# A mixer layer with three attention branches: the 630 DMAs that are not transposes are issued from GpSimd's queue instead of SyncE's

## The chip, the core and the metric

The kernel runs on one core of one Trainium2 chip. The metric is the device time of one execution in microseconds (us). TensorE (PE in the rows) multiplies; its weight loads have rows of their own (PEld). VectorE is DVE, ScalarE is ACT, GpSimd is POOL. SyncE (SP) computes nothing: it issues DMAs, one after the other, and a DMA that waits for something holds up those behind it in the same queue. GpSimd's queue works the same way, but has arithmetic in it as well.

## The reference

One layer of width 1024 over 2048 tokens. The normalised input goes through one wide projection; its columns feed three causal attention branches, a SiLU path for each, and 3072 sigmoid gates:

```python
h = rmsnorm(x, norm_g[l])
proj = h @ w_in[l]
...
pd = p[:, :, 0] - lam * p[:, :, 1]            # differential attention, 4 heads of two maps
s = s + c[:, :, start:end, None] - c[:, :, None, :end]   # forgetting attention, 8 heads
DIL_PATTERNS = ((128, 1), (512, 4), (2048, 16))          # dilated windows, 8 heads
...
y = jnp.stack([ya, yb, yc], axis=2)           # each times silu(its z columns)
branch = jnp.einsum('bsne,nef->bsnf', y, w_branch[l])
merged = jnp.sum(gates * branch, axis=2)
x = x + merged @ w_out[l]
return rmsnorm(x, final_g)
```

## The kernel before

Every product is made in f16 from a high and a low half, so a projection of 128 columns by 512 tokens is 24 matmuls. The work goes through twelve groups of 128 columns of attention output: groups 0 to 3 are differential, 4 to 7 forgetting, 8 to 11 dilated. A tail follows (branch projections, gates, output projection, final norm). In the profile the start and groups 0 and 1 take up to some 280 us, the other differential groups run to about 900 us, the forgetting ones to 1680, the dilated ones to 2380, and the tail to the end.

Inside a group, score jobs are interleaved with projection work for this group and the next (value, SiLU path, gates, query and key). The order of each engine's instructions is set by a scheduler from the program and its own estimates of durations. Tiles come from pools with few slots, and an instruction that writes into a used slot waits for the slot's last reader.

A score job: TensorE makes the scores (L661, L662; L1095, L1098 in dilated groups), VectorE adds the bias and takes the maximum into a tile `e` (L696, L1109), ScalarE takes the exponential (L710, L1118), both split it into halves (L727, L728), a DMA transpose brings it into `eT` (L736), and TensorE multiplies it by the values (L718, L721). There are 5 slots for `e` and 6 for `eT`.

All DMAs are issued from SyncE's queue, `Q`. The transposes are those of `eT`, of the values `v` (L546), of the SiLU path `zt` (L574) and, in the tail, of `u` (L1321). The other DMAs are weight loads `w` (L324, 3 slots; VectorE takes their maximum next, L304), gate stores `gd` (L594, from 3 slots `gs` that the `v` and `z` evictions use too), copies `q2` of query halves (L668, L669, L1004, L1005), the row of decays `R` (L942), outputs `ud` (L1231), loads `gt`, `w_b`, `wo` of the tail, and four kinds of the dilated groups: values to DRAM and back in strided order (`vd` L549, then `v1` L1038 and `v2` L1040), results of the strided patterns to DRAM (`od` L1155, from 3 slots that hold `ro` and `o`), their statistics (`sp` L1170) and their loads back (`o1`, `o2`, L1195). Loads of x, stores of the result and a few small ones have a place of their own in the program and are not touched.

GpSimd's arithmetic: it adds the halves of `zt` into `z` (L575), masks a bias tile `bl` for each forgetting job (L964), copies statistics into `ro` (L1146), and after each group multiplies and adds what finishes it. After a dilated group g that is `post_dil`, which runs beside the jobs of group g+1: eight rounds of multiplying `y` (L1192) and the loaded `o1` and `o2` (L1197), adding them (L1198), and a product with `z` every second round (L1213). Only when it is over can the next group's `z` be written, since `y` and `z` share 3 slots.

Of the kernel before, what the change touches and what calls it, by code (L numbers as in the profile page):

```python
# [19 lines left out]
P = 128  # L20
# [136 lines left out]
def tile_hybrid_trunk(  # L157
# [14 lines left out]
    V, A, G, T, Q = nc.vector, nc.scalar, nc.gpsimd, nc.tensor, nc.sync  # L172

# [145 lines left out]
    def w_load(pieces, name):  # L319
        wt = w_tile(f"w_{name}")  # L320
        stg = wt[:, 256:].rearrange("p (k c) -> p k c", k=KC)
        o = 0
        for c, w in pieces:
            Q.dma_start(stg[:, :, o:o + w], w2[:, c:c + w].rearrange("(k p) c -> p k c", p=P))  # L324
            o += w
        return wt
# [202 lines left out]
    def fill_v(gr):  # L529
# [3 lines left out]
        for t4 in range(4):  # L533
# [13 lines left out]
            if gr["br"] == 2:  # L547
                for a in range(2):
                    Q.dma_start(gr["vd"][512 * t4:512 * t4 + 512, a].rearrange("(b p) c -> p b c", p=P), vt[:, 4 * a:4 * a + 4])  # L549
# [33 lines left out]
    def gate_unit(i, tg):  # L583
# [10 lines left out]
        Q.dma_start(gd[i // 4][i % 4][:, 512 * tg:512 * tg + 512], t)  # L594
# [69 lines left out]
    def make_q2(gr, u, i):  # L664
# [3 lines left out]
        Q.dma_start(t[0:64], stk[64:128, 0, ts])  # L668
        Q.dma_start(t[64:128], stk[0:64, 0, ts])  # L669
# [265 lines left out]
    def prologue_fox(gr):  # L935
        gr["R"] = []
        for u in range(2):
# [4 lines left out]
            Q.dma_start(R, csd[NB * h:NB * h + NB].rearrange("b t -> (b t)").unsqueeze(0).to_broadcast([P, S]))  # L942
# [56 lines left out]
    def prologue_dil(gr):  # L999
        i = gr["i"]  # L1000
        q2 = []
        for u in range(2):
            t = e_tile(f"q2_{gr['n']}_{u}", (P, S), F16)
            Q.dma_start(t[0:64], gr["stk"][u][64:128, 0])  # L1004
            Q.dma_start(t[64:128], gr["stk"][u][0:64, 0])  # L1005
# [23 lines left out]
    def load_v_dil(gr):  # L1029
        gr["vp"] = [None, None, None]  # L1030
        for p in (1, 2):
# [3 lines left out]
            if p == 1:  # L1035
                vs = gr["vd"].rearrange("(j x c r) a e -> j c x (r a e)", j=4, c=4, r=d)
                for j in range(4):
                    Q.dma_start(vv[:, j], vs[j])  # L1038
            else:
                Q.dma_start(vv[:, 0], gr["vd"].rearrange("(i r) a c -> i (r a c)", r=d))  # L1040
            gr["vp"][p] = vt

    def jobs_dil(gr):
# [17 lines left out]
        def job(p, bs):  # L1061
# [59 lines left out]
            def T_():  # L1121
                eh = transpose_tile(hold["e"], widths, 2.0 ** 14, name)

                def pv():
                    seen = set()
                    for h in range(0, len(bs), 2):
# [24 lines left out]
                        if p > 0:  # L1151
# [3 lines left out]
                            Q.dma_start(v, ro)  # L1155
# [10 lines left out]
    def post_dil(gr):  # L1166
        y, s1, n = gr["y"], gr["s1"], gr["n"]
        sp = bl_tile(f"sp_{n}").rearrange("p (a b c) -> p a b c", a=2, c=4)
        for p in (1, 2):
            Q.dma_start(sp[:, p - 1], gr["od"][p].rearrange("(b p) c -> p b c", p=P)[:, :, P:P + 4])  # L1170
# [17 lines left out]
        for i in range(8):  # L1188
# [4 lines left out]
            for p in (1, 2):  # L1193
                o = ro_tile(f"o{p}_{n}_{i}")[:, :256].rearrange("p (b c) -> p b c", b=2)
                Q.dma_start(o, gr["od"][p].rearrange("(b p) c -> p b c", p=P)[:, sl, :P])  # L1195
# [5 lines left out]
    def post(gr):  # L1201
# [25 lines left out]
        for t4 in range(4):  # L1227
# [3 lines left out]
            Q.dma_start(ud[gr["br"]][:, t4, gr["i"]], yh[:, ts])  # L1231
# [93 lines left out]
    def load_gate(n):  # L1325
        if n < 24:
            j, tg = divmod(n, 4)
            gts[n] = xpool.tile([P, 4, 512], F32, tag=f"xT1_{tg}", name=f"gt_{n}")
            Q.dma_start(gts[n], gd[j][:, :, 512 * tg:512 * tg + 512].rearrange("f p t -> p f t"))
# [9 lines left out]
    def prep_b(br, j):  # L1339
# [3 lines left out]
        Q.dma_start(sf.rearrange("p (k c) -> p k c", k=4), w_branch[0, br, :, 256 * j:256 * j + 256].rearrange("(k p) c -> p k c", p=P))  # L1343
# [93 lines left out]
    def load_out(c):  # L1437
        t = w_tile(f"wo_{c}") if c < W_SLOTS else e_tile(f"wo_{c}", (P, 1280))
        j, a = divmod(c, 2)
        Q.dma_start(t[:, 256:].rearrange("p (k c) -> p k c", k=4), w_out[0, 512 * a:512 * a + 512, 256 * j:256 * j + 256].rearrange("(k p) c -> p k c", p=P))  # L1440
# [237 lines left out]
```

## Time and profile before

| what | us |
|---|---|
| median of 3 runs | 2783.12 (2778.27 to 2783.22) |
| the profiled execution | 2802.34 |
| its span, first to last instruction | 2800.6 |

The profiled execution lies 19 us above the median of the runs; every duration below is from it. A busy share is an average over stages with different limits, so stages are read apart. A wait is booked to what ended last before it.

### The profile page before, as it was taken

How to read it: one execution, taken by the hardware profiler on the slowest of the kernel's cores; microseconds unless marked ns; L12 is line 12 of the kernel's file. 1: busy time of each engine (PE TensorE's matmuls, PEld its weight loads, DVE VectorE, ACT ScalarE, POOL GpSimd, SP SyncE). 2: the span in 40 equal slices, each digit the busy share in tenths (PEclk: the TensorE clock that was granted, in tenths of full speed). 3: DMA queues.
4: the chain of work that ended last, by engine and by line, in shares of the span. 5: the costliest groups of instructions: out<-in, count | busy, mean ns of one | idle time of the engine just before them, and what ended most of it. 6: DMA issues, size and time to landing. Idle time of an engine off the chain costs nothing.

```text
span 2800.6 us, 48432 instructions
## 1 busy us (share of the span) xinstructions
PE 2634.3 (94%) x16264; PEld 1378.4 (49%) x16264; DVE 2088.7 (75%) x7120; ACT 1669.5 (60%) x3642; POOL 383.4 (14%) x565
## 2 busy tenths in 40 slices
PE   7999999999999999999999998998979887999998
PEld 4455445455455444454455444544545444444555
DVE  8687978977977868778778776667667665678855
ACT  6466666656566666666676656756758577435311
POOL 0000200200102102102111120132041310400000
PEclk9899999989999999999999999998989998999999
DMA  4345445444455787887886878679687799764222
GB/s 159 74 88 111 89 92 108 99 83 110 90 105 112 140 162 143 159 156 148 150 167 131 153 137 145 133 149 162 138 158 156 139 204 230 212 187 137 95 100 76
DMA packets 981834, 377.02 MB, mean 135 GB/s; under 512 B 842824, under 2 KB 939856, under 8 KB 980048
## 3 DMA queue, kind: packets, MB, share of 16 engines
q1 hardware_dynamic: 981584, 373.93, 63.3%
q8 instruction: 127, 2.08, 0.3%
q14 instruction: 123, 1.01, 0.1%
HBM read 118.14 MB, written 59.05 MB: 63 GB/s over the span
## 4 chain that ended last, share of the span: by engine, by line
PE 58%; DVE 13%; DMA 12%; ACT 8%; issue 5%; SPq 2%; POOL 1%; DVEq 0%; ACTq 0%; POOLq 0%
PE pq_g L385 12%; PE pg L385 11%; PE pbr L385 9%; DMA eT_g<-e_g 6%; PE pz_g L385 5%; PE pout L1485 4%; PE po_g L718 3%; PE pv_g L385 3%; PE s_g L661 3%; PE s_g L662 3%; ACT e_g L1118 2%; DVE e_g L728 2%; PE pout L1486 2%; DVE e_g L696 2%; PE po_g L721 2%
## 5 line engine op out<-in xcount | busy, mean ns | idle before, releaser
L385 PE MATMUL pg<-xT,w_g 128*128 128x512 f16 x2304 | 582.9, 394 | 4.4 <-ACT gs L593 2.8
L710 ACT ACTIVATE e_g<-e_g,nm_g,c_g 128x1024 f32<-128x1024 f32 (+7 forms) x384 | 377.6, 984 | 251.4 <-DVE nm_g L704 218.4
L385 PE MATMUL pq_g<-xT,w_q 128*128 128x512 f16 x1536 | 388.4, 399 | 15.5 <-DVE stk_g L416 14.8
L728 DVE SCALAR_TENSOR_TENSOR e_g<-e_g 128x512 f16<-128x512 f32 (+2 forms) x480 | 316.4, 669 | 89.0 <-ACT e_g L727 86.4
L718 PE MATMUL po_g<-v_g,eT_g 128*128 128x128 f16 (+1 forms) x2232 | 315.4, 236 | 34.6 <-DMA eT_g<-e_g 16.8
L385 PEld LDWEIGHTS <-w_g 128*128 128x128 f16 x2304 | 223.6, 101 | 244.3 <-issue 13.9
L727 ACT ACTIVATE e_g<-e_g 128x512 f16<-128x512 f32 (+2 forms) x480 | 265.9, 569 | 91.3 <-DVE e_g L728 86.7
L385 PE MATMUL pz_g<-xT,w_z 128*128 128x512 f16 x1152 | 288.4, 390 | 6.5 <-DVE stk_g L416 5.3
L721 PE MATMUL po_g<-v_g,eT_g 128*128 128x64 f16 (+1 forms) x2232 | 293.6, 201 | 0.0
L385 PE MATMUL pv_g<-xT,w_v 128*128 128x512 f16 x1152 | 283.2, 395 | 2.8 <-DVE vs_g L545 1.4
L1118 ACT ACTIVATE e_g<-e_g,nm_g,c_g 128x256 f32<-128x256 f32 (+1 forms) x384 | 207.8, 543 | 111.0 <-DVE nm_g L1114 109.0
L385 PE MATMUL pbr<-u,w_b 128*128 128x512 f16 x1152 | 264.9, 393 | 4.1 <-ACT gs L593 1.9
L718 PEld LDWEIGHTS <-eT_g 128*128 128x128 f16 x2232 | 211.2, 100 | 87.0 <-DMA eT_g<-e_g 25.2
L661 PE MATMUL s_g<-stk_g 128*128 128x512 f16 (+3 forms) x640 | 228.1, 358 | 25.1 <-DVE pm_g L696 24.7
L721 PEld LDWEIGHTS <-eT_g 128*128 128x128 f16 x2232 | 206.5, 99 | 78.7 <-issue 21.7
L385 PEld LDWEIGHTS <-w_q 128*128 128x128 f16 x1536 | 148.7, 102 | 178.1 <-DVE stk_g L416 16.7
L696 DVE CUSTOM_DVE_ANT_0 e_g<-s_g,bias_g 128x512 f32<-128x512 f32 (+3 forms) x320 | 190.3, 605 | 60.8 <-DMA eT_g<-e_g 39.1
L662 PE MATMUL s_g<-stk_g,q_g 128*128 128x512 f16 (+3 forms) x640 | 229.0, 360 | 0.2 <-issue 0.2
L696 DVE CUSTOM_DVE_ANT_0 e_g<-s_g,R_g 128x512 f32<-128x512 f32 (+3 forms) x288 | 171.5, 597 | 43.9 <-DMA eT_g<-e_g 29.7
L385 PEld LDWEIGHTS <-w_b 128*128 128x128 f16 x1152 | 115.3, 100 | 146.6 <-issue 8.1
L385 PEld LDWEIGHTS <-w_v 128*128 128x128 f16 x1152 | 114.8, 101 | 134.9 <-issue 7.9
L1485 PE MATMUL pout<-wo,acc 128*128 128x512 f16 x512 | 172.7, 389 | 0.0
(476 smaller groups left out, 4331.7 us busy)
## 6 DMA issues: line engine op xcount, KB each, us to landing
gd<-gs SPq DMA_DIRECT2D x96, 256.0 KB, 2.7
gt<-gd SPq DMA_DIRECT2D x24, 1024.0 KB, 5.2
w_g<-in_w_in_dram SPq DMA_DIRECT2D x24, 512.0 KB, 4.1
ud<-y_g SPq DMA_DIRECT2D x48, 256.0 KB, 3.1
eT_g<-e_g SPq DMA_TRANSPOSE x640, 3.2
od_g<-ro_g SPq DMA_DIRECT2D x64, 132.0 KB, 2.3
xb<-in_x_dram SPq DMA_DIRECT2D x16, 512.0 KB, 6.5
q_g<-stk_g SPq DMA_DIRECT2D x128, 64.0 KB, 2.3
```

What stands on the lines that cost most here:

```text
L385: T.matmul(dst, l, r, start=(i == 0), stop=(i == n - 1))
L661: behind_read(T.matmul(ps, stk[:, 0, qsl], stk[:, 1, ksl], start=True, stop=False))
L662: T.matmul(ps, q2s, stk[:, 1, ksl], start=False, stop=True)
L696: rd = V.tensor_tensor_reduce(out=et[ch // 2][:, o + a:o + a + sw], in0=ps[:, a:a + sw], in1=b, scale=1.0, scalar=-3e38, op0=ALU.add, op1= ...
L710: A.activation(e[:, 256:256 + w], e[:, 256:256 + w], AF.Exp, bias=nm, scale=gr["c"][u], accum_out=den_of(i))
L718: ins = T.matmul(po, eh, vv, start=first, stop=False)
L721: T.matmul(po[:, 0], el, vv[:, 0], start=False, stop=last)
L727: A.activation(h[:, :w], f, AF.Copy, scale=scale)
L728: V.scalar_tensor_tensor(h[:, w:], f, scale, h[:, :w], op0=ALU.mult, op1=ALU.subtract)
L1118: A.activation(eu, eu, AF.Exp, bias=nm[:, 2 * a + u:2 * a + u + 1], scale=gr["c"][u], accum_out=sm[:, a, 2 + u:3 + u])
L1485: T.matmul(po, ah, wo[un][k], start=k == 0, stop=False)
L1486: T.matmul(po[:, 0], al, wo[un][k][:, 0], start=False, stop=k == KC - 1)
```

## The change

A name `RQ` for GpSimd's DMA queue is added, and the DMAs named above that are not transposes are issued through it: 630 of the 1437. What they move, and what waits for them, stays the same. The loads of x, `dl`, `g8`, `fw`, `fb`, `gb`, `fg`, the store `csd`, the stores of the result and all transposes stay with SyncE.

```diff
--- before.py
+++ after.py
@@ -170,6 +170,7 @@
     V, A, G, T, Q = nc.vector, nc.scalar, nc.gpsimd, nc.tensor, nc.sync
+    RQ = nc.gpsimd
 
@@ -321,7 +322,7 @@
         for c, w in pieces:
-            Q.dma_start(stg[:, :, o:o + w], w2[:, c:c + w].rearrange("(k p) c -> p k c", p=P))
+            RQ.dma_start(stg[:, :, o:o + w], w2[:, c:c + w].rearrange("(k p) c -> p k c", p=P))
             o += w
@@ -546,7 +547,7 @@
                 for a in range(2):
-                    Q.dma_start(gr["vd"][512 * t4:512 * t4 + 512, a].rearrange("(b p) c -> p b c", p=P), vt[:, 4 * a:4 * a + 4])
+                    RQ.dma_start(gr["vd"][512 * t4:512 * t4 + 512, a].rearrange("(b p) c -> p b c", p=P), vt[:, 4 * a:4 * a + 4])
                 if t4 == 3:
@@ -591,7 +592,7 @@
             A.activation(t, pd, AF.Copy)
-        Q.dma_start(gd[i // 4][i % 4][:, 512 * tg:512 * tg + 512], t)
+        RQ.dma_start(gd[i // 4][i % 4][:, 512 * tg:512 * tg + 512], t)
 
@@ -665,8 +666,8 @@
         ts = slice(512 * i, 512 * i + 512)
-        Q.dma_start(t[0:64], stk[64:128, 0, ts])
-        Q.dma_start(t[64:128], stk[0:64, 0, ts])
+        RQ.dma_start(t[0:64], stk[64:128, 0, ts])
+        RQ.dma_start(t[64:128], stk[0:64, 0, ts])
         return t
@@ -939,7 +940,7 @@
             R = bias_tile(f"R_{gr['n']}_{u}")
-            Q.dma_start(R, csd[NB * h:NB * h + NB].rearrange("b t -> (b t)").unsqueeze(0).to_broadcast([P, S]))
+            RQ.dma_start(R, csd[NB * h:NB * h + NB].rearrange("b t -> (b t)").unsqueeze(0).to_broadcast([P, S]))
             A.activation(R, R, AF.Copy, scale=nic)
@@ -1001,8 +1002,8 @@
             t = e_tile(f"q2_{gr['n']}_{u}", (P, S), F16)
-            Q.dma_start(t[0:64], gr["stk"][u][64:128, 0])
-            Q.dma_start(t[64:128], gr["stk"][u][0:64, 0])
+            RQ.dma_start(t[0:64], gr["stk"][u][64:128, 0])
+            RQ.dma_start(t[64:128], gr["stk"][u][0:64, 0])
             q2.append(t)
@@ -1035,9 +1036,9 @@
                 for j in range(4):
-                    Q.dma_start(vv[:, j], vs[j])
+                    RQ.dma_start(vv[:, j], vs[j])
             else:
-                Q.dma_start(vv[:, 0], gr["vd"].rearrange("(i r) a c -> i (r a c)", r=d))
+                RQ.dma_start(vv[:, 0], gr["vd"].rearrange("(i r) a c -> i (r a c)", r=d))
             gr["vp"][p] = vt
@@ -1152,7 +1153,7 @@
                             v = v[:, r_, j:j + 2] if p == 1 else v[:, r_:r_ + 2, j]
-                            Q.dma_start(v, ro)
+                            RQ.dma_start(v, ro)
                         yield
@@ -1167,7 +1168,7 @@
         for p in (1, 2):
-            Q.dma_start(sp[:, p - 1], gr["od"][p].rearrange("(b p) c -> p b c", p=P)[:, :, P:P + 4])
+            RQ.dma_start(sp[:, p - 1], gr["od"][p].rearrange("(b p) c -> p b c", p=P)[:, :, P:P + 4])
         yield 2500
@@ -1192,7 +1193,7 @@
                 o = ro_tile(f"o{p}_{n}_{i}")[:, :256].rearrange("p (b c) -> p b c", b=2)
-                Q.dma_start(o, gr["od"][p].rearrange("(b p) c -> p b c", p=P)[:, sl, :P])
+                RQ.dma_start(o, gr["od"][p].rearrange("(b p) c -> p b c", p=P)[:, sl, :P])
                 ov = o.rearrange("p b (u c) -> p b u c", u=2)
@@ -1228,7 +1229,7 @@
             V.scalar_tensor_tensor(yh[:, ts, 1], z[:, ts], s, yh[:, ts, 0], op0=ALU.mult, op1=ALU.subtract)
-            Q.dma_start(ud[gr["br"]][:, t4, gr["i"]], yh[:, ts])
+            RQ.dma_start(ud[gr["br"]][:, t4, gr["i"]], yh[:, ts])
             yield 1000
@@ -1326,7 +1327,7 @@
             gts[n] = xpool.tile([P, 4, 512], F32, tag=f"xT1_{tg}", name=f"gt_{n}")
-            Q.dma_start(gts[n], gd[j][:, :, 512 * tg:512 * tg + 512].rearrange("f p t -> p f t"))
+            RQ.dma_start(gts[n], gd[j][:, :, 512 * tg:512 * tg + 512].rearrange("f p t -> p f t"))
 
@@ -1340,7 +1341,7 @@
         sf = wt[:, 256:1280]
-        Q.dma_start(sf.rearrange("p (k c) -> p k c", k=4), w_branch[0, br, :, 256 * j:256 * j + 256].rearrange("(k p) c -> p k c", p=P))
+        RQ.dma_start(sf.rearrange("p (k c) -> p k c", k=4), w_branch[0, br, :, 256 * j:256 * j + 256].rearrange("(k p) c -> p k c", p=P))
         return prep_b2(br, j, wt, sf, name)
@@ -1437,7 +1438,7 @@
         j, a = divmod(c, 2)
-        Q.dma_start(t[:, 256:].rearrange("p (k c) -> p k c", k=4), w_out[0, 512 * a:512 * a + 512, 256 * j:256 * j + 256].rearrange("(k p) c -> p k c", p=P))
+        RQ.dma_start(t[:, 256:].rearrange("p (k c) -> p k c", k=4), w_out[0, 512 * a:512 * a + 512, 256 * j:256 * j + 256].rearrange("(k p) c -> p k c", p=P))
 
```

The scheduler orders all engines anew. Two places are shown. The first is GpSimd early in group 9, inside `post_dil` of group 8 (`o1_g8_2` is the load of its round 2; `v1_g9`, `v2_g9` and `vd_g9` are the strided values of group 9; names in brackets are the semaphores waited for, DMASW those of GpSimd's DMAs and DMAHW those of SyncE's). Before:

```order
L1197 TENSOR_TENSOR o2_g8_1_22848<-o2_g8_1_22848,wc_g8_22763 128x256 [waits DMAHW2_49]
L1198 TENSOR_TENSOR y_g8_20546<-y_g8_20546,o2_g8_1_22848 128x256 [waits Pool_49]
L1213 TENSOR_TENSOR z_g8_21263<-z_g8_21263,y_g8_20546 128x512 [waits Pool_49]
L1197 TENSOR_TENSOR o1_g8_2_22898<-o1_g8_2_22898,wc_g8_22763 128x256 [waits DMAHW5_49]
L1197 TENSOR_TENSOR o2_g8_2_22902<-o2_g8_2_22902,wc_g8_22763 128x256 [waits DMAHW6_49]
L1198 TENSOR_TENSOR y_g8_20546<-y_g8_20546,o1_g8_2_22898 128x256 [waits Pool_49]
L1198 TENSOR_TENSOR y_g8_20546<-y_g8_20546,o2_g8_2_22902 128x256 [waits Pool_49]
L1197 TENSOR_TENSOR o1_g8_3_22944<-o1_g8_3_22944,wc_g8_22763 128x256 [waits DMAHW2_49]
L1197 TENSOR_TENSOR o2_g8_3_22948<-o2_g8_3_22948,wc_g8_22763 128x256 [waits DMAHW3_49]
L1198 TENSOR_TENSOR y_g8_20546<-y_g8_20546,o1_g8_3_22944 128x256 [waits Pool_49]
```

With the change:

```order
L1039 DMA v1_g9_23095<-vd_g9_22716 128x1x1024 [waits DMASW0_49]
L1198 TENSOR_TENSOR o2_g8_1_22848<-o2_g8_1_22848,wc_g8_22763 128x256 [waits DMASW1_49]
L1198 TENSOR_TENSOR o1_g8_2_22898<-o1_g8_2_22898,wc_g8_22763 128x256 [waits DMASW2_49]
L550 DMA vd_g9_22716<-v_g9_3_23089 128x4x128 [waits DMAHW7_49]
L550 DMA vd_g9_22716<-v_g9_3_23089 128x4x128
L1039 DMA v1_g9_23095<-vd_g9_22716 128x1x1024 [waits DMASW5_49,DMASW4_49,DMASW3_49]
L1198 TENSOR_TENSOR o2_g8_2_22902<-o2_g8_2_22902,wc_g8_22763 128x256 [waits DMASW6_49]
L1199 TENSOR_TENSOR y_g8_20546<-y_g8_20546,o2_g8_1_22848 128x256 [waits Pool_49]
L1199 TENSOR_TENSOR y_g8_20546<-y_g8_20546,o1_g8_2_22898 128x256 [waits Pool_49]
L1039 DMA v1_g9_23095<-vd_g9_22716 128x1x1024 [waits DMASW2_49,DMASW1_49]
L1041 DMA v2_g9_23100<-vd_g9_22716 128x4096
L1196 DMA o1_g8_3_22944<-od1_g8_20548 128x2x128 [waits Pool_49]
```

The rounds of `post_dil` stood behind one another; now the store of the last quarter of group 9's values, which waits for a transpose, and the loads that wait for that store stand between round 2 and the loads of round 3.

The second place is SyncE at the same point (`eT_g9_0_4_1` is the second transpose of a score job of group 9). Before:

```order
L736 DMA_TRANSPOSE eT_g9_0_4_0_23031<-e_g9_0_4_22778 128x8x128 [waits DMAHW3_49,DVE_49]
L1195 DMA o1_g8_5_23053<-od1_g8_20548 128x2x128 [waits DMAHW4_49,Pool_49]
L1195 DMA o2_g8_5_23057<-od2_g8_20549 128x2x128 [waits Pool_49]
L1195 DMA o1_g8_6_23074<-od1_g8_20548 128x2x128 [waits DMAHW7_49,DMAHW6_49,Pool_49]
L546 DMA_TRANSPOSE v_g9_3_23089<-vs_g9_3_23088 128x8x128 [waits DVE_49]
L1038 DMA v1_g9_23095<-vd_g9_22716 128x1x1024 [waits DMAHW0_49]
L736 DMA_TRANSPOSE eT_g9_0_4_1_23035<-e_g9_0_4_22778 128x8x128 [waits DMAHW1_49,DVE_49]
L736 DMA_TRANSPOSE eT_g9_0_6_0_23151<-e_g9_0_6_22885 128x8x128 [waits DMAHW2_49,PE_49]
```

With the change:

```order
L547 DMA_TRANSPOSE v_g9_3_23089<-vs_g9_3_23088 128x8x128 [waits DMASW6_49,DMAHW7_49,DMASW5_49,DVE_49]
L737 DMA_TRANSPOSE eT_g9_0_2_1_22941<-e_g9_0_2_22734 128x8x128 [waits DMAHW0_49,DVE_49,PE_49]
L737 DMA_TRANSPOSE eT_g9_0_4_0_23031<-e_g9_0_4_22778 128x8x128 [waits DMAHW1_49,DVE_49,PE_49]
L737 DMA_TRANSPOSE eT_g9_0_4_1_23035<-e_g9_0_4_22778 128x8x128 [waits DMAHW2_49,DVE_49,PE_49]
L737 DMA_TRANSPOSE eT_g9_0_6_0_23151<-e_g9_0_6_22885 128x8x128 [waits DMAHW3_49,DMAHW5_49,DVE_49,PE_49]
L737 DMA_TRANSPOSE eT_g9_0_6_1_23155<-e_g9_0_6_22885 128x8x128 [waits DMAHW4_49,DVE_49,PE_49]
```

The loads of `o` and `v1` between the transposes are gone from SyncE, and the transposes follow one another directly.

## Rows read from the trace of the kernel before

**Rows 1.** The page: busy us of TensorE, and the chain that ended last.
```profile
PE 2634.3 (94%) x16264; PEld 1378.4 (49%) x16264; DVE 2088.7 (75%) x7120; ACT 1669.5 (60%) x3642; POOL 383.4 (14%) x565
...
PE 58%; DVE 13%; DMA 12%; ACT 8%; issue 5%; SPq 2%; POOL 1%; DVEq 0%; ACTq 0%; POOLq 0%
PE pq_g L385 12%; PE pg L385 11%; PE pbr L385 9%; DMA eT_g<-e_g 6%; PE pz_g L385 5%; PE pout L1485 4%; PE po_g L718 3%; PE pv_g L385 3%; PE s_g L661 3%; PE s_g L662 3%; ACT e_g L1118 2%; DVE e_g L728 2%; PE pout L1486 2%; DVE e_g L696 2%; PE po_g L721 2%
```

**Rows 2.** Windows by stage: busy us (count) by engine, clock, DMA share, GB/s.
```profile
0.00:280.00 280.00, 260.42 (x1340) 133.64 (x1341) 209.83 (x728) 167.39 (x329) 11.40 (x16) 0.94 0.46 108
280.00:900.00 620.00, 602.64 (x3614) 313.61 (x3613) 513.25 (x1645) 382.83 (x761) 68.87 (x63) 0.93 0.48 99
900.00:1680.00 780.00, 741.05 (x5108) 384.61 (x5107) 605.39 (x2087) 508.68 (x1037) 127.23 (x198) 0.94 0.77 149
1680.00:2380.00 700.00, 617.38 (x4117) 337.14 (x4114) 464.14 (x1872) 472.61 (x1269) 142.98 (x244) 0.91 0.81 161
2380.00:2800.00 420.00, 412.82 (x2093) 209.42 (x2091) 296.10 (x793) 137.96 (x248) 32.89 (x45) 0.94 0.44 135
```

**Rows 3.** Timeline of SyncE, forgetting groups: start us, us, what.
```profile
1199.74 0.53 SPq L594 DMA_DIRECT2D gd<-gs  x1
...
1204.67 1.24 SPq L736 DMA_TRANSPOSE eT_g<-e_g  x1
```

**Rows 4.** DMA issues, whole run: count, KB, median us to landing.
```profile
w_g<-in_w_in_dram SPq DMA_DIRECT2D x24, 512.0 KB, 4.1
...
eT_g<-e_g SPq DMA_TRANSPOSE x640, 3.2
```

**Rows 5.** Waits, whole run: us in total, times, longest us.
```profile
PE po_g L718 <- DMA eT_g<-e_g: 16.8, 17, 2.7
...
DVE e_g L696 <- DMA eT_g<-e_g: 91.2, 63, 4.3
...
DVE amp_g L304 <- DMA w_g<-in_w_in_dram: 26.1, 17, 5.0
```

**Rows 6.** Windows of three stretches, early in groups 9 to 11.
```profile
1820.00:1890.00 70.00, 65.89 (x413) 34.30 (x412) 45.02 (x176) 39.35 (x109) 26.51 (x42) 0.93 0.71 150
2030.00:2100.00 70.00, 55.89 (x333) 28.82 (x332) 46.77 (x170) 36.61 (x99) 34.45 (x46) 0.88 0.82 159
2170.00:2240.00 70.00, 62.14 (x380) 31.87 (x379) 42.94 (x161) 37.87 (x105) 24.31 (x39) 0.91 0.75 141
```

**Rows 7.** DMA issues between 1820 and 1890 us.
```profile
o_g<-od_g SPq DMA_DIRECT2D x13, 128.0 KB, 2.5
...
sp_g<-od_g SPq DMA_DIRECT2D x2, 32.0 KB
v_g<-vs_g SPq DMA_TRANSPOSE x4, 3.1
```

**Rows 8.** Timeline of SyncE, early in group 9.
```profile
1875.69 2.65 SPq L1195 DMA_DIRECT2D o_g<-od_g  x3
...
1887.12 1.23 SPq L546 DMA_TRANSPOSE v_g<-vs_g  x1
...
1898.45 0.48 SPq L324 DMA_DIRECT2D w_g<-in_w_in_dram  x1
```

**Rows 9.** Tile pv_g on TensorE: duration ns, first to last start us.
```profile
L385 PE MATMUL pv_g<-xT,w_v x96: 385/388/399, 1849.5 to 1874.2; 128*128 128x512 f16 x96
```

**Rows 10.** Timeline of VectorE at the same place.
```profile
1879.52 0.68 DVE L545 SCALAR_TENSOR_TENSOR vs_g<-pv_g,vs_g 128x512 f16<-128x512 f32 x1
```

**Rows 11.** Timeline of GpSimd, group 9 [idle us before].
```profile
1917.68 1.27 POOL L1213 TENSOR_TENSOR z_g<-z_g,y_g 128x512 f32<-128x512 f32 x1
...
1938.85 1.16 POOL L575 TENSOR_TENSOR z_g<-zt_g 128x512 f32<-128x512 f16 x1 [5.51 <-DVE sw_g L199]
```

**Rows 12.** GpSimd by line: busy us, mean ns, idle us before.
```profile
L1213 POOL TENSOR_TENSOR z_g<-z_g,y_g 128x512 f32<-128x512 f32 x48 | 65.1, 1372 | 0.9
...
L1197 POOL TENSOR_TENSOR o_g<-o_g,wc_g 128x256 f32<-128x256 f32 x64 | 44.1, 701 | 80.9 <-DMA o_g<-od_g 80.9
```

## Prediction

> **What bounds the kernel now.** I read the page first: TensorE is busy for 2634.3 us of the 2800.6 of the span, so 166 us are all that any change of the DMAs can take away, unless it shortens matmuls [rows 1]. The windows by stage say where those 166 us lie: 20 in the start, 17 in the differential groups, 39 in the forgetting ones, 83 in the dilated ones, 7 in the tail [rows 2]. So the dilated groups are the place to look at. There the DMA engines are busy at 0.81, GpSimd at 143 us of 700, and the granted clock is lowest, at 0.91 against 0.94 in the two stages beside it (2.4 GHz is full speed).
>
> The chain that ended last comes next. It is 58% TensorE; 12% of it, 336 us, are DMAs under way, 5.8 to 6% of the span of them, some 165 us, the transposes of `eT`; and 2%, 56 us, is SyncE's queue itself [rows 1]. The waits say who feels the transposes: TensorE itself for 16.8 us only, VectorE for 91.2 us at L696, where a slot of `e` comes free late; and VectorE waits for gate weights for 26.1 us [rows 5]. These waits of VectorE have part of its idle quarter as cover.
>
> Last, I looked at one place in the dilated groups closely, since the order of instructions changes most there. TensorE starts the last matmul of group 9's values at 1874.2 us [rows 9], which frees a weight slot; the load that wants this slot is issued at 1898.45 [rows 8], 24 us later. It had stood behind transposes. In the same way the last transpose of `v` could go when VectorE's split ends at 1880.2 (1879.52 + 0.68) [rows 10], and goes at 1887.12 [rows 8]. A single queue does hold things up here.
>
> **The change, part by part.** *What SyncE loses.* A plain DMA takes 0.53 us to issue there, a transpose 1.24 [rows 3]. The 630 that leave took 630 x 0.53 = 334 us; the 640 transposes of `eT` take 794 [rows 4]. So what leaves is 30% of the sum, and if the 56 us of SyncE on the chain shrink by that share, the gain is **17 us**. I choose this share over the whole 56, because the transposes still wait for one another.
>
> *What an issue costs on GpSimd.* No row of before has a DMA on GpSimd, so the price c is bounded. Below stands SyncE's 0.53 us [rows 3]. Above stands 1.37 us, GpSimd's own costliest common operation, a 128x512 product [rows 12], which lies near a transpose's 1.24. I take 1.0, the middle of the two rounded up, since GpSimd's queue is also shared with arithmetic.
>
> *Where that cost is felt.* Of the 336 us of DMAs on the chain, the transposes of `eT` take 165; I leave out some 35 more for loads of x, stores and other transposes that stay, which is a choice. The rest, 136 us, at about 3 us for each landing (2.5 to 4.1 us) [rows 4, 7], is some 45 links. Each becomes longer by c - 0.53 = 0.47 us: **+21 us**. Weight loads are the clearest of them, since VectorE already waits for them when they land [rows 5]. The bounds: nothing at c = 0.53, +38 us at 1.37.
>
> *GpSimd's own work in the dilated groups.* Between 1820 and 1890 us there are 41 DMAs that move, in nine kinds from 13 of `o` to 2 of `sp` [rows 7], beside 26.5 us of arithmetic [rows 6]. At c = 1.0 that makes 67.5 us of work in 70; the two like stretches have 34.5 and 24.3 us of arithmetic and nearly as many DMAs. GpSimd goes from nearly idle to full, but does not overflow. The order shows what suffers: the loads of round 3 of `post_dil` now stand behind `v1` and `v2`, and so behind the last transpose of `v`. Before, they went at 1875.69 [rows 8]. Now that transpose may go at 1880.2, lands 3.1 us later [rows 7], its two stores take 2 us and about 2.5 to land, and the two loads 2 us more: round 3 begins at about 1889.8, 14 us later. The rest of `post_dil` is ten loads (10 us), ten products of 0.70 us [rows 12] and ten sums of about the same, three products of 1.37 us [rows 12], and five waits for a landing of some 1.5 us each: 36 us, so it ends at about 1926. It ended at 1918.95, and the next user of its slot, the first part of the next `z`, came at 1938.85 [rows 11]: 20 us of cover, of which 7 are used. If this cover were gone, the SiLU path would hold its `gs` slots and TensorE would stop behind the evictions. I take 2 us for each of the three posts that run beside dilated groups, for stores of `od` held behind loads: **+6 us**. The bounds are nothing and, at c = 1.37, an overflow of 26.5 + 41 x 1.37 - 70 = 12.7 us in each: 38.
>
> *What is hidden.* The `q2` copies, `ud`, and in the tail `gt` and `w_b` move too. TensorE idles for only 7 us of the tail's 420 [rows 2], so the tail's loads are covered by its matmuls; should that cover go, its 24 loads `gt` would cost 0.47 us each, 11 us in all. In the forgetting groups GpSimd has 127 us of arithmetic in 780 [rows 2], room enough for the DMAs.
>
> *The sum.* -17 + 21 + 6 = +10 us on the profiled execution's 2802.3, or 2812. That execution lies 19 us above the median of the runs, 2783.1, so for a median I say **2793 us**.
>
> The Trainium skill, "DMA: Bandwidth & Descriptors", section "Issuing engines are not separate DMA queues", says that DMAs of all issuing engines run on the same 16 DMA engines, and that issuing from more than one saves only the sequencer's time. It speaks against any larger gain: by it the most would be the -17. The trace agrees in so far as the DMA engines are already at 0.81 in the dilated groups [rows 2].
>
> **The rivals.** *Faster.* The moved DMAs no longer stand behind transposes (24 us in the one case above), transposes no longer behind them, and the price on GpSimd is near 0.53. Then the links cost nothing, the -17 stays, and half of TensorE's 16.8 us for `eT` [rows 5] goes as well: -25, 2758 us. For it speaks that VectorE's waits for `eT` are the largest of its waits for a DMA; against it, that TensorE waits little for them. It decides where c is under about 0.75 us: there the links cost 10 us, and 17 exceeds 10 + 6.
>
> *GpSimd becomes the bound.* Each issue also has to wait until a VectorE instruction is over, 0.68 us for a common one [rows 10], so that c is 1.7. VectorE is busy for 75% of the span [rows 1], so most issues would meet one. Then the links cost 45 x 1.17 = 53 us and the first stretch overflows by 26.5 + 41 x 1.7 - 70 = 26 us, the three perhaps by 57: 2783 - 17 + 53 + 57 = 2876 us. It decides from c = 1.06, where that stretch is full. Against it: nothing in the trace shows the two engines in each other's way at GpSimd's small arithmetic.
> The Trainium skill, "SBUF — State Buffer", section "SBUF: two separate sides", says that a DMA issued from GpSimd has its descriptors written by GpSimd's cores, and that VectorE in some of its modes shuts them out while it runs. No run here shows it yet.
>
> *Nothing moves.* What SyncE gives and GpSimd takes cancel, or both lie under matmuls: 2783 us. For it speaks that TensorE is busy for 94%.
>
> **How the numbers follow.** About 0.2%, 5.6 us, is what a measurement of this kernel can tell from no change. My forecast, slower by 6 to 30 us, has 0.38; GpSimd as the bound 0.12; faster 0.33; no change 0.17. That makes 0.50 for slower, 0.17 for the same, 0.33 for faster. The forecast's own range is 2789 to 2813. Since both signs have weight, the whole range is 2757, the full gain, to 2845, which is the sum with both upper bounds (-17 + 38 + 38 = +59, 2842); it leaves out the worst half of the bound case.
>
> **What would show it.** Right: DMAs on GpSimd at about 1 us each, GpSimd near 1000 us in all (383 + 630), `v1` and `v2` ahead of round 3 in its timeline, SyncE free between transposes, and TensorE's idle time a little larger in the dilated groups, smaller in the forgetting ones. Wrong: a price at either bound; TensorE's idle time falling below 83 us in the dilated groups; or long waits of VectorE at L304 or L696 for something that GpSimd does late, which would make the loss larger in groups that I hold to be covered.

## The result and the profile after

The change makes the kernel slower: 2925.61 us (median of 4 runs, 2917.33 to 2934.57) beside 2782.11 us for the kernel before on the same chip (4 runs). The ratio is 1.0519, with a 95% interval of 1.048 to 1.0558. The forecast was 2793 us, and the range ended at 2845: the sign was right, the size was missed by 133 us, and none of the three terms holds the loss.

One remark on the base. The profiled execution of [rows 1 to 12] ran at a mean granted clock of 0.932, while the timed runs of the same kernel beside the experiments had 0.973 to 0.980. So that the clock isn't taken for an effect of the change, the profile after is read here beside that of a **control**: the kernel before with its own order of instructions written out. It takes 2777.03 us (10 runs), 1.0000 of the kernel before (0.9991 to 1.0009), and its profiled execution has the clock 0.978. How an order is written out stands with the first experiment.

The page of the kernel after, busy us and the DMA queues (packets, MB, share of 16 engines), which answers to [rows 1]:

```profile
span 2918.1 us, 48611 instructions
...
PE 2603.5 (89%) x16264; PEld 1366.6 (47%) x16264; DVE 2106.2 (72%) x7120; ACT 1668.5 (57%) x3642; POOL 795.7 (27%) x1195
...
q1 hardware_dynamic: 752048, 210.31, 42.2%
q0 software_dynamic: 51680, 163.64, 20.5%
```

The same lines of the control:

```profile
PE 2560.1 (92%) x16264; PEld 1356.0 (49%) x16264; DVE 2089.5 (75%) x7120; ACT 1667.3 (60%) x3642; POOL 384.2 (14%) x565
...
q1 hardware_dynamic: 981584, 373.93, 63.7%
```

TensorE has idle time of 2918.1 - 2603.5 = 314.6 us after, and 2773.7 - 2560.1 = 213.6 in the control. So of the 144 us between the two spans 101 are new idle time, and 43 are the same 16264 matmuls taking longer. The busy share does not show what is wrong: no engine became busier than TensorE. The queues show what is new: one queue of DMAs, q1, became two, and the new one, q0, GpSimd's, holds its 163.64 MB in few, large packets (3166 bytes in the mean, where the packets that left q1 held 163.62 MB in 229536, 713 bytes in the mean).

The windows by stage, as in [rows 2], with each kernel's own bounds of the stages. After:

```profile
0.00:283.30 283.30, 251.79 (x1333) 129.33 (x1334) 204.76 (x718) 165.28 (x328) 46.11 (x66) 0.98 0.42 106
283.30:887.30 604.00, 564.15 (x3460) 295.80 (x3459) 500.08 (x1585) 366.57 (x726) 133.50 (x172) 0.97 0.47 97
887.30:1725.60 838.30, 745.04 (x5157) 389.01 (x5156) 622.66 (x2144) 522.82 (x1067) 215.66 (x345) 0.97 0.75 140
1725.60:2510.10 784.50, 656.48 (x4291) 353.17 (x4290) 491.70 (x1897) 476.57 (x1280) 327.98 (x513) 0.91 0.79 148
2510.10:2918.10 408.00, 386.00 (x2030) 199.26 (x2028) 286.98 (x780) 137.22 (x243) 72.41 (x100) 0.98 0.46 136
```

The control, its last three stages:

```profile
868.40:1650.40 782.00, 729.54 (x5158) 383.54 (x5157) 616.99 (x2146) 524.33 (x1070) 123.56 (x198) 0.99 0.79 150
1650.40:2367.90 717.50, 620.52 (x4228) 342.42 (x4226) 476.36 (x1891) 476.65 (x1279) 150.62 (x251) 0.95 0.80 160
2367.90:2773.70 405.80, 398.08 (x2091) 205.52 (x2091) 295.10 (x792) 137.86 (x247) 33.20 (x45) 0.99 0.44 140
```

The forgetting groups lose 56 us (782.0 to 838.3) and the dilated ones 67 (717.5 to 784.5); start, differential groups and tail lose 21 together. GpSimd is busy for 216 of 838 and 328 of 784 us: nowhere full.

The waits, as in [rows 5] (us in total, times, longest us). After:

```profile
DVE e_g L697 <- DMA eT_g<-e_g: 162.5, 75, 11.1
DVE e_g L1110 <- DMA eT_g<-e_g: 103.6, 24, 15.0
PEld L719 <- DMA eT_g<-e_g: 72.8, 36, 6.9
PE po_g L719 <- DMA eT_g<-e_g: 57.6, 28, 6.4
...
DVE amp_g L305 <- DMA w_g<-in_w_in_dram: 14.4, 9, 4.1
DVE amp_ug L305 <- POOL z_g L1214: 14.0, 4, 3.9
```

The control:

```profile
DVE e_g L696 <- DMA eT_g<-e_g: 95.0, 69, 4.4
DVE e_g L1109 <- DMA eT_g<-e_g: 52.7, 18, 8.2
...
DVE amp_g L304 <- DMA w_g<-in_w_in_dram: 28.5, 17, 5.5
PE po_g L718 <- DMA eT_g<-e_g: 21.8, 23, 2.9
...
DVE amp_ug L304 <- POOL z_g L1213: 10.3, 6, 5.9
```

The waits of TensorE and VectorE that grew most are for `eT`, the transposes that did not move. TensorE's own went from 21.8 us to 57.6, VectorE's at the slots of `e` from 95.0 to 162.5 and from 52.7 to 103.6. The next to grow is TensorE's wait at the scores of the dilated groups (L1095, L1096 after) for VectorE to have read earlier ones, from 10.5 to 30.6 us. VectorE's wait for gate weights, which moved, became smaller. I followed every gap of TensorE over 0.06 us back along the waits to its start, in both traces: the part of the gaps in which a transpose of `eT` was under way rose from 40.0 to 100.4 us, that of weight loads `w_g` fell from 4.4 to 1.4, and that of GpSimd rose from 0.3 to 7.4.

The DMA issues after, as in [rows 4] and [rows 7] (count, KB, median us to landing):

```profile
w_g<-in_w_in_dram POOLq DMA_DIRECT2D x24, 512.0 KB, 4.9
...
eT_g<-e_g SPq DMA_TRANSPOSE x640, 3.4
...
o_g<-od_g POOLq DMA_DIRECT2D x64, 128.0 KB, 4.2
```

A median hides this effect: 3.2 us became 3.4 (the page has it from those transposes alone whose landing it could tell). What the trace also holds is the last semaphore update of each transpose. From these, over all 640, the mean from issue to landing is 3.48 us in the control and 4.25 after; over 6 us took 26 and 85 of them; the longest after took 18.8. The time that a transpose waits for its issue, once VectorE's split (the later of the two halves that it reads) is over, went from 1.76 us to 1.53. By stage the landing went from 3.37 to 4.00 in the forgetting groups and from 3.94 to 5.42 in the dilated ones. Transposes during whose flight hardly any other DMA's bytes moved (up to 4 KB) landed in 3.18 us in the control (340 of them) and 3.17 after (278); where over 256 KB of others moved, they took 4.54 us in the control (121 of them) and 5.99 after (226).

One such place, in the first dilated group of the kernel after. The timeline of SyncE and of GpSimd:

```profile
1772.53 24.36 SPq L737 DMA_TRANSPOSE eT_g<-e_g  x5
...
1777.00 0.73 POOL L1039 DMA_DIRECT2D v_g<-vd_g  x1 [2.89 <-DMA vd_g<-v_g]
1777.73 0.56 POOL L1041 DMA_DIRECT2D v_g<-vd_g  x1
```

And TensorE there, a row of its timeline and the window of these 20 us:

```profile
1786.57 0.29 PE L719 MATMUL po_g<-v_g,eT_g 128*128 128x128 f16 x1 [5.67 <-DMA eT_g<-e_g]
...
1774.00:1794.00 20.00, 14.33 (x63) 5.96 (x60) 8.04 (x26) 8.57 (x19) 1.39 (x3) 0.71 1.22 146
```

GpSimd issues the last load of `v1` (256 KB) and `v2` (1024 KB) while SyncE is at these transposes. SyncE needs 24.4 us for five of them, 21.1 of it for the issues themselves, where five take 6.2 at the price of [rows 3]; two single issues take 6.5 and 9.5 us. TensorE stops for 5.67 us. The granted clock of the window is 0.71, so part of it was spent at 1.2 GHz.

### The profile page after: what moved, and what is told of

The parts are those of the page before. It is cut to its first block, busy times and chain, and to the rows that moved or that the text cites. A ratio compares the mean times of both kernels' runs of the same rounds, so it can differ in the third digit from the quotient of the medians.

```text
span 2918.1 us, 48611 instructions
## 1 busy us (share of the span) xinstructions
PE 2603.5 (89%) x16264; PEld 1366.6 (47%) x16264; DVE 2106.2 (72%) x7120; ACT 1668.5 (57%) x3642; POOL 795.7 (27%) x1195
## 3 DMA queue, kind: packets, MB, share of 16 engines
q0 software_dynamic: 51680, 163.64, 20.5%
## 5 line engine op out<-in xcount | busy, mean ns | idle before, releaser
L386 PE MATMUL pg<-xT,w_g 128*128 128x512 f16 x2304 | 572.7, 391 | 14.9 <-DVE zs_g L574 10.3
L719 PE MATMUL po_g<-v_g,eT_g 128*128 128x128 f16 (+1 forms) x2232 | 316.1, 235 | 75.1 <-DMA eT_g<-e_g 57.6
L386 PE MATMUL pv_g<-xT,w_v 128*128 128x512 f16 x1152 | 273.1, 386 | 11.7 <-DVE vs_g L546 5.0
L386 PE MATMUL pbr<-u,w_b 128*128 128x512 f16 x1152 | 258.1, 385 | 10.6 <-ACT gs L594 4.7
L1110 DVE CUSTOM_DVE_ANT_0 e_g<-s_g,bd_g 128x128 f32<-128x128 f32 (+1 forms) x408 | 123.4, 348 | 134.4 <-DMA eT_g<-e_g 103.6
## 6 DMA issues: line engine op xcount, KB each, us to landing
xb<-in_x_dram SPq DMA_DIRECT2D x16, 512.0 KB, 10.3
```

The costliest lines, as they stand in the source:

```text
L386: T.matmul(dst, l, r, start=(i == 0), stop=(i == n - 1))
L719: ins = T.matmul(po, eh, vv, start=first, stop=False)
L1110: rd = V.tensor_tensor_reduce(out=eo, in0=pi, in1=bi, scale=1.0, scalar=-3e38, op0=ALU.add, op1=ALU.max, accum_out=am[:, c:c + 1] if cut e ...
```

## The experiments

Where a part of the change is tried alone, the order of PE, DVE, ACT and SyncE is that of the kernel before, written out, so that only the queue differs. An excess is the ratio less one, times the time of the kernel before measured beside it.

**The control: the kernel before, its order written out.** Edges that set the order of issue, and no wait, chain the instructions of each engine:

```diff
+def pin_order(tc):
...
+            if prev is not None:
+                tc.add_manual_dep(ins, prev, mybir.DependencyInfo(mybir.DependencyClass.NoSync, mybir.DependencyReason.DATA), reason="pin")
+            prev = ins.name
```

> The kernel before, all DMAs on SyncE, with its own order written out as in the other runs. Every theory: no change, 2775 to 2795 us. Its profile is the base for those of the other runs, at the clock that their executions have.

Measured: 1.0000 (0.9991 to 1.0009), as above. Writing the order out costs nothing.

**Queue or order.** The change moves queues, and the scheduler then orders all engines anew. Two kernels take these apart. The first has the queues of after with the order of before (GpSimd's arithmetic and the moved DMAs each keep theirs); the second has everything on SyncE with the order of after.

```diff
+    RQ = nc.gpsimd
...
+        pin_order(tc)
```

> The queues of the changed kernel (630 DMAs on GpSimd) with the order of before written out for TensorE, VectorE, ScalarE and SyncE's transposes; on GpSimd its arithmetic and the moved DMAs keep the order they had among themselves. Three theories. Shared engines: DMAs of a second queue run beside the transposes on the same 16 DMA engines, and the transposes land later (3.2 us alone, 5 to 9 us where over 256 KB of other DMAs move meanwhile), so the loss stays: 2900 to 2940 us, landing of eT above 3.8 us on average. GpSimd's queue: the moved DMAs stand behind waits of GpSimd's arithmetic and of each other; the loss stays as well: 2880 to 2950 us. New order: the loss comes from the scheduler's other order on TensorE, VectorE and ScalarE; then it goes with that order: 2770 to 2800 us.

> All DMAs on SyncE as before, but TensorE, VectorE, ScalarE and GpSimd's arithmetic in the order of the changed kernel, and SyncE's transposes and other DMAs each in the order they have there. Shared engines and GpSimd's queue: without the second queue the loss is gone, 2770 to 2810 us. New order: the loss stays with the order, 2890 to 2940 us. A value between says that both have a part.

Measured: 2933.89 us, 1.0546 (1.052 to 1.0572), for the queues with the old order; 2814.15 us, 1.0109 (1.0092 to 1.0126), for the new order on one queue. So it is the queue, +152 us of excess; its interval overlaps that of the kernel after. The new order costs 30 us by itself on one queue, so at that order the second queue adds some 114 (1.0519 less 1.0109); beside two queues the order costs nothing that shows. The order has its part in what was read above, too: on one queue with the new order TensorE's gaps hold 59.3 us of `eT` transposes in flight (the control 40.0, after 100.4), although these land after 3.45 us in the mean. Of the 77 us by which TensorE idles longer with two queues at that order, 41 are `eT`.

**The queues by themselves.** The layer is left out. Seven stretches of 24 transposes like those of `eT`, issued in pairs; a plain DMA waits until the pair before has landed. The transposes run alone, then with 12 stores of 256 KB from SyncE, GpSimd and ScalarE, then with 6 loads of 1 MB from each.

```diff
+    def stores_gpsimd():
+        for k in range(12):
+            if k:
+                seen(k - 1, st[k % 3])
+            pair(k)
+            store(G, "g", k)
```

> Leaves out the whole layer; the output is a constant. Seven stretches of 24 transposes of 128x1024 f16 each from SyncE, one stretch after the other: alone; with a 256 KB store after each pair, issued by SyncE, by GpSimd, by ScalarE; with a 1 MB load after every second pair, issued by the same three. Shared engines: with SyncE alone a transpose that is ahead in the queue is not delayed by what comes behind it, so it lands in about 3.2 to 4 us; with the same DMAs from GpSimd or ScalarE it lands in 4 to 5 us beside stores and 7 to 10 beside the loads, while the stretch as a whole takes about as long. GpSimd's queue: landings stay within 0.5 us of those with SyncE, whichever engine issues.

Measured: the DMA issues of the first four stretches (count, KB, median us to landing):

```profile
eT<-src SPq DMA_TRANSPOSE x24, 3.3
...
gd<-st SPq DMA_DIRECT2D x12, 256.0 KB, 2.5
eT<-src SPq DMA_TRANSPOSE x24, 3.2
...
gd<-st POOLq DMA_DIRECT2D x12, 256.0 KB, 3.9
eT<-src SPq DMA_TRANSPOSE x24, 4.3
...
gd<-st ACTq DMA_DIRECT2D x12, 256.0 KB, 3.3
eT<-src SPq DMA_TRANSPOSE x24, 4.1
```

With the loads the means from issue to landing of a transpose are 4.64 us (loads from SyncE), 5.12 (GpSimd) and 5.42 (ScalarE). On one queue a store leaves the transposes alone: they land after 3.2 us, as without it. From a second queue, whichever engine has it, both get slower: transposes 4.1 to 4.3 us, stores 3.3 and 3.9 instead of 2.5. So it is no matter of GpSimd's price (0.55 us for these stores, SyncE's 0.53, ScalarE's 0.33), but of two queues that share the 16 DMA engines. With loads of 1 MB one queue is no full shelter: a transpose behind a load lands late there as well (4.64 us in the mean beside 3.33 alone, longest 6.9), and the second queue adds 0.5 to 0.8 us to that. The 7 to 10 us that were expected beside the loads did not come.

The Trainium skill, "DMA: Bandwidth & Descriptors", section "Queues, rings and completion order", says that each DMA engine takes its queues in turn, a packet at a time. The trace agrees in so far as each of the two queues delays the other, and the stores from one do not.

**Parts of the change.** Four kernels move one kind each: the gates (`gd`, `gt`, 120 DMAs), the weights (`w`, `w_b`, `wo`, 122), the copies (`q2`, `R`, `ud`, 200), the kinds of the dilated groups (188).

```diff
-        Q.dma_start(gd[i // 4][i % 4][:, 512 * tg:512 * tg + 512], t)
+        RQ.dma_start(gd[i // 4][i % 4][:, 512 * tg:512 * tg + 512], t)
```

```diff
-            Q.dma_start(stg[:, :, o:o + w], w2[:, c:c + w].rearrange("(k p) c -> p k c", p=P))
+            RQ.dma_start(stg[:, :, o:o + w], w2[:, c:c + w].rearrange("(k p) c -> p k c", p=P))
```

```diff
-        Q.dma_start(t[0:64], stk[64:128, 0, ts])
+        RQ.dma_start(t[0:64], stk[64:128, 0, ts])
```

```diff
-                            Q.dma_start(v, ro)
+                            RQ.dma_start(v, ro)
```

> The order of before as in the first run; of the moved DMAs only the gate stores gd (96, 24 MB) and the loads gt of the tail (24, 24 MB) go to GpSimd, the others stay with SyncE. Shared engines: the loss goes by the bytes that run beside transposes, here some 24 of the 122 MB that were moved beside them (the 24 MB of gt run after the last score job): 20 to 45 us of the 150. GpSimd's queue: gd stands between GpSimd's masks, which wait for VectorE, so gs slots come free late: 30 to 60 us, with waits of ScalarE for gs slots in the trace.

> The same with the weight loads alone on GpSimd (122 with those of the tail; 38 MB beside score jobs, in pieces of 256 and 512 KB). Shared engines: 30 to 60 us. GpSimd's queue: these loads wait only for a free slot and are few, so 10 us at most, or a gain, since they no longer stand behind transposes.

> The same with the copies of query halves, the rows R and the outputs ud alone on GpSimd (200 DMAs, 32 MB). They are due tens of us after they are issued, so nothing waits for them. Shared engines: still 25 to 50 us, since they run beside transposes. GpSimd's queue: no loss, within 10 us.

> The same with the DMAs of the dilated groups alone on GpSimd (vd, v1, v2, od, sp, o: 188 DMAs, 28 MB, all between 1680 and 2400 us). Shared engines: 25 to 50 us, all in that stretch. GpSimd's queue: this is where one DMA stands behind the other (v1 behind vd, rounds of loads behind v1 and v2), so most of the 150 us: 70 to 130.

Measured: gates 2803.33 us, 1.0063 (1.0041 to 1.0086); weights 2839.97, 1.0202 (1.0183 to 1.0221); copies 2797.51, 1.005 (1.0032 to 1.0067); dilated kinds 2826.82, 1.0159 (1.0134 to 1.0184). Every part loses. Worked out as excess: 18, 56, 14 and 44 us, 132 in all, beside 152 for the whole with the same order. Gates and copies lose less than the 20 and 25 us that were expected at least. The loss does not go by the bytes alone: the copies move 32 MB and cost 14 us, the weights 38 MB beside score jobs and cost 56.

The weights lose most, and are the clearest case, since their own waits do not grow. Waits of that kernel:

```profile
DVE e_g L697 <- DMA eT_g<-e_g: 125.5, 69, 6.4
PEld L719 <- DMA eT_g<-e_g: 64.4, 35, 10.1
...
PE po_g L719 <- DMA eT_g<-e_g: 52.9, 28, 9.6
DVE amp_g L305 <- DMA w_g<-in_w_in_dram: 13.9, 6, 4.1
```

122 loads that VectorE waits for no longer than before (gate weights 13.9 us beside 28.5, all weights `w` 83.9 beside 87.2) raise TensorE's wait for `eT` from 21.8 to 52.9. The mean landing of `eT` rose from 3.48 to 3.84 us, and over 6 us took 57 instead of 26. In TensorE's gaps `eT` has 76.3 us instead of 40.0, `w_g` 3.1 instead of 4.4.

**The price of a late transpose.** If late landings are the cause, transposes made late in another way must cost as much. The kernel before, with the order written out, gets a 4-byte DMA from SyncE right ahead of 368 of the 640 transposes. It reads what the split wrote, so it waits as the transpose does, and adds its own issue.

```diff
+                if c == 0:
+                    a = Q.dma_start(dd[:, len(tiny):len(tiny) + 1], e[0:1, w // 2:w // 2 + 1])
```

> The kernel before with one DMA of 4 bytes, which waits for the same splits, right ahead of each score tile's first transpose on SyncE (368 of the 640 transposes; the second one of a tile stands behind). No second queue. It delays a transpose by one issue, 0.5 us. Landing theory: in the runs so far the time rose with the mean landing of eT (3.47 us before, 3.57 with the gates moved, 3.84 with the weights, 3.63 with the copies) by some 100 to 150 us for each us, so half a us more for most transposes costs 40 to 80 us. If the later landing is mostly hidden and the loss comes from elsewhere: under 20 us.

Measured: 2820.12 us, 1.0159 (1.0144 to 1.0175), an excess of 44 us. The wait from split to issue rose from 1.76 to 2.31 us and the landing did not grow (3.42 beside 3.48). So a transpose came later by 0.50 us (both together) to 0.56 (the wait alone), and 44 us over these are an estimate of 79 to 88 us of time for each us. The 4-byte DMAs also hold up the plain DMAs behind them on SyncE, which this price contains.

The forgetting groups allow the closest comparison, since the kernel with the old order on two queues has the same sequence of matmuls there (the same matmul by its number bounds the stage; means over the 320 transposes of groups 4 to 7):

| kernel | wait to issue + landing, us | stage longer by, us | of it idle |
|---|---|---|---|
| control | 1.78 + 3.37 = 5.15 | | |
| 4-byte DMAs, one queue | 2.50 + 3.33 = 5.83 | 35.2 | 26.7 |
| two queues, old order | 1.72 + 3.98 = 5.70 | 42.0 | 24.7 |
| weights alone | 1.87 + 3.72 = 5.59 | 30.7 | 18.8 |

Transposes that come 0.68 us later by their issue cost 35 us, and 0.55 us later by their landing cost 42. So a late transpose costs time of this size, but a late landing costs half as much again for each us of the mean (76 us beside 52; 70 with the weights alone). One reason may be that late landings come in lumps: over 6 us took 8 of the 320 in the control, 5 with the 4-byte DMAs, 31 on two queues and 26 with the weights. That is argued and not tried. Lateness is not the only way to lose here: the new order on one queue makes the stage 29.2 us longer with transposes only 0.11 us later.

**The dilated groups.** Two more kernels divide the fourth part: the strided values (`vd`, `v1`, `v2`, 52 DMAs) and the results (`od`, `sp`, `o1`, `o2`, 136).

```diff
-                    Q.dma_start(vv[:, j], vs[j])
+                    RQ.dma_start(vv[:, j], vs[j])
```

```diff
-                Q.dma_start(o, gr["od"][p].rearrange("(b p) c -> p b c", p=P)[:, sl, :P])
+                RQ.dma_start(o, gr["od"][p].rearrange("(b p) c -> p b c", p=P)[:, sl, :P])
```

> The order of before; of the DMAs of the dilated groups only vd, v1 and v2 (52) go to GpSimd. Shared engines: v1 and v2 are loads of 256 KB and 1 MB that now run beside transposes; eT lands later in the dilated groups (4.4 us or more on average against 3.9), 15 to 30 us. GpSimd's queue: these wait for one another in any queue, 10 us at most.

> The order of before; of the DMAs of the dilated groups only od, sp and o (136) go to GpSimd, where the arithmetic of post_dil waits for them. Shared engines: 16 MB in pieces of 128 KB, 5 to 15 us. GpSimd's queue: the loads o stand behind products in the same queue, a post gets some 10 us longer, and the one of the last group, which no score jobs cover, holds up the branch products of the tail: 15 to 35 us, with waits of TensorE behind z between 2430 and 2500 us.

Measured: values 2792.79 us, 1.0064 (1.0047 to 1.0082), an excess of 18; results 2796.01, 1.007 (1.0046 to 1.0094), 19. With the values the transposes' part of TensorE's gaps grows from 40.0 us to 51.5, and what of it lies beside `v1` and `v2` in flight from 3.7 to 19.0; the longest landing is 15.3 us. With the results the mechanism is another one. Waits of that kernel:

```profile
DVE amp_ug L305 <- POOL z_g L1214: 37.0, 8, 10.5
...
PE pq_g L386 <- DVE stk_g L417: 20.3, 12, 10.0
```

Its timeline early in group 9, of GpSimd, VectorE and TensorE:

```profile
1897.43 0.60 POOL L1198 TENSOR_TENSOR o_g<-o_g,wc_g 128x256 f32<-128x256 f32 x1 [3.94 <-DMA o_g<-od_g]
...
1900.11 1.27 POOL L1214 TENSOR_TENSOR z_g<-z_g,y_g 128x512 f32<-128x512 f32 x1
...
1901.42 0.69 DVE L305 TENSOR_REDUCE amp_ug<-z_g 128x1 f32<-128x512 f32 x1 [2.78 <-POOL z_g L1214]
...
1902.82 0.69 DVE L417 SCALAR_TENSOR_TENSOR stk_g<-pq_g,stk_g 64x512 f16<-64x512 f32 x1
...
1903.57 1.89 PE L386 MATMUL pq_g<-xT,w_q 128*128 128x512 f16 x4 [10.03 <-DVE stk_g L417]
```

The loads of `post_dil` come later to GpSimd, its product with `z` ends later, VectorE's maximum over that product stands in VectorE's queue and waits for it, the eviction `stk` stands behind that, and TensorE stops for 10.03 us. VectorE's wait for the product is 2.78 us of this pause; shortly before, it had waited 3.10 us for a weight load from SyncE, so the pause is not all GpSimd's. Over the whole run GpSimd's part of TensorE's gaps rose from 0.3 to 11.9 us and that of the transposes fell from 40.0 to 30.9. The wait was expected in the tail, between 2430 and 2500 us, and stands here beside score jobs. With all four dilated kinds this wait of VectorE is 79.4 us, beside 10.3 in the control. In the full change it is 14.0 only; that there the transposes make the jobs late first, so that the product is in time for them, is argued and not tried.

## Why the prediction was wrong

**The step that failed** is *What SyncE loses* together with *Where that cost is felt*. The first counts the transposes that stay as gaining, since their queue gets shorter; the second gives a longer way to the moved DMAs alone. The landing of `eT`, 165 us of the chain by the prediction's own reading, was left as it was. This is what changed: 3.48 to 4.25 us in the mean, and TensorE's gaps hold 60 us more of transposes in flight. By the price of the 4-byte DMAs (79 to 88 us for each us), 0.77 us are an estimate of 61 to 68 us, and 0.54 us (0.77 less the 0.23 won in waiting) 43 to 48 of the 144 us between the two profiled spans. So the mean lateness at that price carries a third of the loss; the gaps, read directly, carry more. I had the rows for the danger: the DMA engines at 0.77 and 0.81 in the two stages that lost most [rows 2]. I read the rule that the prediction cites from the Trainium skill, "DMA: Bandwidth & Descriptors", section "Issuing engines are not separate DMA queues", as "no large gain". That DMAs of all issuing engines run on the same 16 engines has a second side here: a short transpose that others wait for shares them with long loads that nobody waits for. One queue had kept most of them out of its way (3.2 us beside stores from one queue, 4.1 to 4.3 from a second).

**The -17.** The plain DMAs do leave SyncE, as foretold, and the wait from split to issue fell from 1.76 to 1.53 us (to 1.46 with the old order). At the price of the 4-byte DMAs 0.23 us are an estimate of 18 to 20 us, so the term may well be there, under a larger loss; no run shows it by itself, and none of the parts gains. Its sum took each transpose at 1.24 us, 794 in all; the 640 issues took 891 us in the trace of before, which makes the share 28% and the term 16.

**The price on GpSimd**, c = 1.0, was too high. The rows of GpSimd by line (busy us, mean ns, idle before):

```profile
L595 POOL DMA_DIRECT2D gd<-gs x96 | 54.6, 569 | 301.9 <-ACT gs L594 221.5 <-ACT y_g L977 21.7 <-ACT y_g L815 10.8
...
L1196 POOL DMA_DIRECT2D o_g<-od_g x64 | 46.5, 727 | 5.5 <-DMA od_g<-ro_g 4.9 <-POOL y_g L1199 0.6
...
L325 POOL DMA_DIRECT2D w_g<-in_w_in_dram x24 | 22.3, 928 | 137.1 <-PE pq_g L386 57.7 <-DVE e_g L809 27.8 <-PE pv_g L386 23.4
...
L1171 POOL DMA_DIRECT2D sp_g<-od_g x8 | 9.4, 1177 | 11.3 <-DMA od_g<-ro_g 9.6 <-ACT ro_g L1150 1.5 <-DVE w_g L318 0.3
```

Over all 630 it is (795.7 - 384.2) / 630 = 0.65 us, under the 0.75 below which the *faster* rival was to decide. By that step the change should have gained: the *faster* rival was nearer with the price, and fell by the landing of `eT` as the forecast did. *GpSimd becomes the bound* fell with c = 1.7.

**GpSimd's own work in the dilated groups.** `v1` and `v2` do stand ahead of round 3. Of the three posts beside dilated groups two are no longer for it (43.6 and 43.5 us from the first to the last product with `z`, in the control 44.5 and 45.8) and the third is (50.9 instead of 38.9); 16 to 25 us of cover up to the next `z` stay. But this cover, 20 us up to the next user of the slot of `z`, was the wrong one. With the results alone on GpSimd, the first to wait is VectorE, at L305, in whose queue the jobs stand behind. The cost of +6 is 19 us for the results and 44 for all dilated kinds where these move alone; in the full change it can't be told from the transposes'. GpSimd is not full: 328 of 784 us.

**What is hidden.** The forgetting groups, held covered because GpSimd has room there, lost 56 us. The cover was counted for the engine that took the DMAs, not for the DMA engines. The sign named for this, a loss in the groups held covered, is what came, though by waits for the transposes and not for GpSimd.

**The clock** has no term in the sum, and 43 of the 144 us are TensorE's busy time. In the trace after, 42 stretches (257 us) run at 1.2 of 2.4 GHz, in the control 21 (123 us), and in the window shown above one of them begins during the 5.67 us pause. These stretches hold 182 us of matmul time after and 91 in the control. So pauses cost twice in part, once as idle time and once in matmuls at the lower clock.

**The range.** Its ends, 2757 and 2845, lie 1 and 3 us outside of the sums that they are worked out from (2758 and 2842), which makes no difference at 2926 us.

**What stays open.** How the 144 us divide is not settled: the price of the 4-byte DMAs gives the transposes a third, the gaps give them 60 of the 101 us of new idle time, and 19 of these 60 come with the new order on one queue already. Why a late landing costs more than a late issue was not tried. The parts add up to 132 us and the whole with the old order to 152. In that kernel TensorE's gaps hold 42 us of weight loads (`w_g` 20.8, `w_q` 9.7, `w_z` 9.1, others 2.9), more than the 29 by which its part of `eT` grew (40.0 to 68.6); in the control these loads have 5.4, and with the weights alone on GpSimd 6.1. A load that stands behind other kinds in GpSimd's queue would explain this; it was argued from the trace and not tried by itself. With the order of after they have 5.7 us. In the sum for the whole change, 144 - 43 leaves 101 us idle, of which `eT` holds 60 (100.4 - 40.0); VectorE's part grew by 26, GpSimd's and ScalarE's by 7 each, and whether these come from late transposes as well was not settled. ScalarE as the second queue was tried on the queues by themselves only, so that in the layer any second queue would lose is not shown. No version found is faster than the kernel before.

## What to carry to other kernels

Before plain DMAs are given a queue of their own, ask which short DMA the critical engines wait for, and look at its landing, not at the issuing queue: on a second queue, long transfers run beside it instead of behind it, and here one us more for each transpose cost some 80 us of time or more. Look at means and at the longest landings, since the median moved by 0.2 us while 5% were lost. And where cover is claimed, name the first instruction in any in-order queue that waits for the result, and not only the next user of its buffer.

## What the runs showed of the hardware

Two queues delay each other on the same 16 DMA engines, in either kind: 12 stores beside 24 transposes left these at 3.2 us from one queue, and made them 4.3 (GpSimd) and 4.1 us (ScalarE) from a second. Loads of 1 MB delayed them from one queue too, to 4.64 us in the mean. A transpose's issue on SyncE can itself be long: 1.24 us is common, and over 2 us took 71 of the 640 after and 44 in the control, the longest 9.5 and 7.0. DMAs of GpSimd's queue moved in larger packets (3166 bytes in the mean beside 713). An issue on GpSimd took 0.54 to 0.93 us for most kinds and 1.18 for the strided statistics; with VectorE busy for 72% of the span, the longest of the 630 issues took 1.19 us: none showed the long stall that a rival had supposed. With 101 us of new idle time, TensorE's clock stood at 1.2 GHz for 257 us instead of 123, and the same matmuls took 43 us more.
